# One hybrid-attention layer on one core: every attention matmul contracts over 128 rows, by padded or doubled operands

## Chip, cores and metric

The kernel runs on one core of one Trainium2 chip. The metric is the device time of the whole program in microseconds (us), the median of several executions. Lower is better. Two versions are compared: the kernel before, and the same kernel with the change below.

## What is computed

One transformer layer, batch 1, 1024 tokens, width 1024, all in float32. The reference, cut to the lines that matter here:

```python
hn = rms_norm(x, g_mix)
proj = hn @ w_in                      # split into q, k, v of three attention kinds, a convolution, gates
# NSA, 4 heads of 64, one shared key head: compressed (63 keys) + selected + window branches
kc = rms_norm(compress_tokens(kc_tok, pe_k, w1_k, w2_k), g_kc)      # 63 keys
vc = compress_tokens(vc_tok, pe_v, w1_v, w2_v)
sc = einsum('bhqd,bnd->bhqn', qi, kc) * scale                       # ... softmax, mask
o_cmp = einsum('bhqn,bnd->bhqd', p_cmp, vc)
ss = einsum('bhqd,bqkjd->bhqkj', qi, kg) * scale                    # selected blocks
# stick-breaking attention, 4 heads of 64
z = einsum('bhqd,bhsd->bhqs', qi, k) * hd ** -0.5
attn = where(past, exp(log_sigmoid(z) - between), 0.0)              # between: sum over later keys
# dilated attention, 4 heads of 64: three dilations, mixed by their log-sum-exp
groups = rms_norm(concat([o_a, o_b, o_c, o_d]), g_out)
x = x + groups @ w_out
h2 = rms_norm(x, g_ffn)
out = x + (silu(h2 @ w_gate) * (h2 @ w_up)) @ w_down
```

## The kernel before

**Products in three passes.** Float32 products run as fast fp32r matmuls: an operand a is split into a high part (rounded, one copy on ACT) and a low part (the rest, one subtraction on DVE or POOL), and a product is hi·hi + hi·lo + lo·hi, three matmuls into one PSUM bank (lines 235 to 237, in `mm3`).

**Stages.** The input is normalized and transposed; projections, a convolution and the attention kinds follow in the order `n0 n1 c0 pd0 d0 pd1 d1 ps0 s0 c1 ps1 g s1` (n: NSA, pd and d: projections and attention of the dilated kind, ps and s: of the stick-breaking kind, c: convolution, g: gains; each for head pair 0 or 1). Then come the output projection, a second norm, and the feed-forward part, which uses a seven-product scheme on half matrices. Each attention stage loops over 8 query tiles of 128 tokens (`qt`), and over chunks of up to 512 keys.

**Scores.** A head has 64 channels, so a head's query fits in half of the 128 partitions. `q_split` puts the high part of head h in its own half of `Q[h]` and the low part in the other half. `k_split` puts the high part of the key in both halves of `K[h]`, so that one matmul over 128 rows (line 496) gives q_hi·k_hi + q_lo·k_hi. The third product, q_hi·k_lo, is a second matmul over the 64 rows of that head alone (line 497): `K[2]` holds k_lo of head 0 in rows 0 to 63 and of head 1 in rows 64 to 127. For NSA, with one shared key head, `K[2]` holds the low part of the key in both halves, and line 497 also takes only 64 of the rows. `HALF` are the two slices of 64 rows.

**The compressed branch** has 63 keys. Its scores (line 662) go through DVE (line 515), the softmax (ACT line 622, then DVE or POOL line 630), a transpose of 63 columns for each head (line 669), a split (lines 522 and 523), and two matmuls over 63 rows with the values `vcHL` (lines 671 and 672).

**After the scores** the weights of a tile are transposed (lines 542 and 544), split (522 on ACT, 523 on DVE) and multiplied with the values (550 and 551). A helper `qk_pair` takes both SP buffers of PSUM for the two heads of a chunk; ten S2 buffers hold score tiles.

**Order.** `fix_order` plans the order of the instructions on each engine with a list scheduler and pins it. Its table of durations gives every fp32r matmul of n columns the same duration, whatever its rows; a DMA ends about 2 us after its issue there. Projection matmuls of the next stages stand between the attention's matmuls on TensorE (PE). SyncE (SP) issues nearly all DMAs, in its planned order: weight loads `raw`, half copies of keys (line 317), masks and distance tables `W` and `Wsp`, stores `mixd`.

Of the kernel before, what the change touches and what calls it, by code (L numbers as in the profile page):

```python
# [9 lines left out]
F32 = mybir.dt.float32  # L10
F32R = mybir.dt.float32r
# [28 lines left out]
WHB = 12  # L40
# [8 lines left out]
def hybrid(ctx, tc, x, gmix, wa1, wa2, wkv, wcv, wd, wc, bgate, gcols, pe, w1, w2,  # L49
           convw, gout, wout, gffn, wgate, wup, wdown, c_wa, c_wsp, c_wd, c_wc, c_ind, out):  # L50
    nc = tc.nc
# [11 lines left out]
    nc.scalar.preload_act_table_set("natural_log_exp_and_others")  # L63
    ident = cst.tile([128, 128], F32, name="ident")
    make_identity(nc, ident)
    if WARM:
# [19 lines left out]
    nc.vector.memset(blk1r[64:128, 64:128].bitcast(F32), 1.0 / HD)  # L86
    identr = cst.tile([128, 128], F32R, name="identr")
    nc.vector.tensor_copy(identr, ident)
    gates = cst.tile([128, NT, 12], F32, name="gates")
# [44 lines left out]

    # ---------------------------------------------------------------- attention pools
    att = ExitStack()
# [6 lines left out]
    def S2(name="S"):  # L143
        return sm.tile([128, 512], F32, tag="S2", bufs=10, name=name)

    wct = sm.tile([128, 4, 120], F32, tag="wct", bufs=1, name="wct")

# [241 lines left out]

    # ---------------------------------------------------------------- NSA projections  # L390
    ks, kw = qktile("ks"), qktile("kw")
# [30 lines left out]
    ks, kw = (ks[0],) + ks, (kw[0],) + kw  # L422
    for dst, src in ((pet, pe), (wct, c_wc), (go, gout), (cvw, convw)):
        nc.sync.dma_start(dst, src)

    # ---------------------------------------------------------------- compression
    KK, VV = Stile(), Stile()
# [12 lines left out]
    kcT = cst.tile([128, 64], F32, name="kcT")  # L440
    vcHL = cst.tile([64, 128], F32R, name="vcHL")
    for z, src in ((0, KK), (1, VV)):
# [46 lines left out]

    # ---------------------------------------------------------------- attention pieces  # L490
    def qk_pair(Q, K, qt, c0, n, diag=None):
        ps = [SPt(), SPt()]
        qc = slice(qt * 128, (qt + 1) * 128)
        kc_ = slice(c0, c0 + n)
        for h in range(2):
            nc.tensor.matmul(ps[h][:, :n], Q[h][:, qc], K[h][:, kc_], start=True, stop=False)  # L496
            nc.tensor.matmul(ps[h][:, :n], Q[h][HALF[h], qc], K[2][HALF[h], kc_], start=False, stop=diag is None)  # L497
        if diag is not None:
            b = max(0, diag - 128)
            for h in range(2):  # L500
                nc.tensor.matmul(ps[h][:, b:b + 256], identr, tri_[0][:, b + 128 - diag:b + 384 - diag],
                                 start=False, stop=True)
        return ps

    def chunks(j0, L):
# [8 lines left out]
    def reduce_min(S, ps, W, mm, first):  # L514
        nc.vector.tensor_tensor_reduce(S, ps, W, op0=OP.add, op1=OP.min, scale=1.0,  # L515
                                       scalar=3e38 if first else mm, accum_out=mm)
# [85 lines left out]
    def attn_nsa(hp, Q):  # L602
        Wt = [sm.tile([128, T], F32, tag="W", bufs=2, name="W") for _ in range(2)]
        Wsp = [sm.tile([128, 128], F32, tag="Wsp", bufs=2, name="Wsp") for _ in range(2)]
        for h in range(2):
            nc.sync.dma_start(Wt[h], c_wa[2 * hp + h])
            nc.sync.dma_start(Wsp[h], c_wsp[2 * hp + h])
        for qt in range(NT):
# [50 lines left out]
            mm, ll = small()  # L659
            Sc = sm.tile([128, 2, 64], F32, tag="Sc", bufs=2, name="Sc")  # L660
            for h in range(2):
                nc.tensor.matmul(ps[h][:, :63], f(Q[h][:, qc]), kcT[:, :63], start=True, stop=True)
            for h in range(2):
                reduce_min(Sc[:, h, :63], ps[h][:, :63], wct[:, 2 * hp + h, 8 * (7 - qt):8 * (7 - qt) + 63],
                           mm[:, h:h + 1], True)
            norm(0, [[Sc[:, 0, :63]], [Sc[:, 1, :63]]], mm, ll)
            tp = Ttile()
            for h in range(2):
                nc.tensor.transpose(tp[:63, h * 128:(h + 1) * 128], Sc[:, h, :63], ident)
            ph, pl = evac_T(tp, [(63, 0, 256)])  # L670
            nc.tensor.matmul(o[:, :256], vcHL[:63, :], ph[:63, :256], start=True, stop=False)
            nc.tensor.matmul(o[:, :256], vcHL[:63, :], pl[:63, :256], start=False, stop=False)
            five = [(j0, 384, 384), (j0 + 384, 256, 256)]
# [20 lines left out]
    def attn_dil(hp, Q, K, V):  # L694
# [3 lines left out]
        for qp in range(NT // 2):  # L698
# [4 lines left out]
            for j in range(2):  # L703
                qt = 2 * qp + j
                L = 128 * (qt + 1)
                w0 = 128 * (7 - qt)
                chs = chunks(0, L)
                for ci, (c0, w, n) in enumerate(chs):
                    ps = qk_pair(Q, K, qt, c0, n)
                    for h in range(2):  # L710
                        P[h, j, ci] = S2()
                        reduce_min(P[h, j, ci][:, :w], ps[h][:, :w], Wt[h][:, w0 + c0:w0 + c0 + w],
                                   mm[:, 2 * h + j:2 * h + j + 1], ci == 0)
                for h in range(2):
                    i = 2 * h + j
                    for ci, (c0, w, n) in enumerate(chs):
                        S = P[h, j, ci][:, :w]
                        nc.scalar.activation(S, S, AF.Exp, bias=mm[:, i:i + 1], scale=-1.0,
                                             accum_out=ll[:, 4 * ci + i:4 * ci + i + 1])
# [19 lines left out]
    def attn_stick(hp, Q, K, V):  # L739
        for qp in range(NT // 2):  # L740
            P = {}
            car = {}
            for ci in range(qp // 2, -1, -1):
                for j in range(2):
# [3 lines left out]
                    diag = ci == qp // 2  # L748
                    ps = qk_pair(Q, K, qt, c0, max(256, w), w - 128 if diag else None)
                    for h in range(2):  # L750
# [17 lines left out]

    # ---------------------------------------------------------------- short convolution
    def conv(i):  # L770
# [61 lines left out]

    # ---------------------------------------------------------------- output projection, second norm
    x2d = [[dram.tile([128, 512], F32, name=f"x2d{t}{h}") for h in range(2)] for t in range(NT)]
# [152 lines left out]

    # ---------------------------------------------------------------- gate and up
    npf = [0]
# [82 lines left out]

    # ---------------------------------------------------------------- down
    NI = NF // 2
# [15 lines left out]
    first = {}  # L1090
# [90 lines left out]

# ---------------------------------------------------------------- issue order
#
# The engines take their instructions in order, so an instruction that is not ready holds up everything
# behind it. fix_order() plans the order of the traced instructions with a list scheduler (each engine
# takes the first instruction in program order that can start) and pins it with same-engine edges. It
# only picks an order: every wait still comes from the tile framework.

# [349 lines left out]
```

## Time and profile before

| | us |
|---|---|
| median of three runs | 1395.58 (1393.94 to 1396.36) |
| profiled execution, first to last instruction | 1392.6 |
| PE busy in it | 1357.9 (98%) |
| DVE busy | 1020.2 (73%) |
| ACT busy | 739.5 (53%) |
| POOL busy | 590.0 (42%) |
| mean granted TensorE clock | 0.998 of full speed |

All times below are from this one execution and count from its first instruction. The page gives no more of its own time than the span of 1392.6 us, which is 3.0 us under the median of the runs. PE's busy time counts matmuls from their start to a modelled end, and several are in flight at once; how fast PE really goes is read from the distance between the starts of matmuls that follow each other. PEld is the weight load of a matmul, which may run beside the matmul ahead of it. NSA runs from about 100 to 315 us, the dilated attention from 315 to 455 us, and the stick-breaking attention from 455 to 680 us; what follows has no 64-row matmul.

### The profile page before, as it was taken

To read this page: it belongs to the slowest core of one execution; us is meant where nothing else is said; L and a number is where in the kernel's file an instruction comes from. 1 tells how busy PE (TensorE), PEld (TensorE's weight loads), DVE (VectorE), ACT (ScalarE), POOL (GpSimd) and SP (SyncE) were. 2 spreads that over 40 slices of the span, in tenths; PEclk is the share of its full clock that TensorE was granted. 3 is DMA by queue.
4 is the path that set the end of the run, shared out by engine and by line. 5 is a ranking of instruction groups with operands and counts; after the bars stand their busy time and mean duration, and the time that the engine had idled before them with its cause. 6 is when DMAs were issued, how large, how long until landed. Compare 5 with 4: busy or idle time off the path is not lost.

```text
span 1392.6 us, 20585 instructions
## 1 busy us (share of the span) xinstructions
PE 1357.9 (98%) x7101; PEld 1102.9 (79%) x7101; DVE 1020.2 (73%) x1985; ACT 739.5 (53%) x1643; POOL 590.0 (42%) x457
## 2 busy tenths in 40 slices
PE   7999999999999999999989999999999999999998
PEld 6997778878777776888987888888888887888786
DVE  6647778788887777788768778775766665679963
ACT  6436577676766778777765432333332323632531
POOL 5413255442311104252377334453444433564845
PEclk9999999999999999999999999999999999999999
DMA  6510011011121102451345444433233325963434
GB/s 217 171 61 5 5 41 63 15 43 50 46 57 43 39 8 76 129 159 61 127 149 187 144 164 161 144 120 99 91 107 114 114 88 196 335 210 109 138 90 158
DMA packets 84136, 150.96 MB, mean 108 GB/s; under 512 B 8960, under 2 KB 30336, under 8 KB 84032
## 3 DMA queue, kind: packets, MB, share of 16 engines
q1 hardware_dynamic: 83472, 147.82, 32.4%
q0 software_dynamic: 560, 1.84, 0.4%
q8 instruction: 56, 0.92, 0.3%
q14 instruction: 48, 0.39, 0.1%
HBM read 111.08 MB, written 36.44 MB: 106 GB/s over the span
## 4 chain that ended last, share of the span: by engine, by line
PE 83%; DVE 10%; DMA 2%; ACT 2%; issue 2%; POOL 1%; SPq 0%; DVEq 0%; POOLq 0%; ACTq 0%
PE PRp L237 9%; PE PRp L236 9%; PE PRp L235 9%; PE SPp L497 5%; PE PRp L1026 3%; PE PRp L1024 3%; PE PRp L1025 3%; PE SPp L496 3%; PE Op L550 2%; PE Op L551 2%; PE Tp L1026 2%; PE SPp L1025 2%; PE Tp L1025 2%; PE SPp L1026 2%; PE SPp L1024 2%; PE Tp L1024 2%
## 5 line engine op out<-in xcount | busy, mean ns | idle before, releaser
L104 POOL TENSOR_TENSOR wlo<-raw,whi 128x512 fp32r<-128x512 f32 x86 | 118.4, 1386 | 150.5 <-ACT whi L103 108.2
L1013 POOL TENSOR_TENSOR fw<-fraw,fw 128x512 fp32r<-128x512 f32 x50 | 68.6, 1372 | 158.2 <-ACT fw L1012 158.1
L523 DVE TENSOR_TENSOR ptl<-Tp,pth 128x512 fp32r<-128x512 f32 (+2 forms) x204 | 106.2, 533 | 31.9 <-ACT pth L522 29.4
L522 ACT ACTIVATE pth<-Tp 128x512 fp32r<-128x512 f32 (+2 forms) x204 | 93.4, 473 | 68.0 <-PE Tp L544 51.3
L1012 ACT ACTIVATE fw<-fs 128x512 fp32r<-128x512 f32 x88 | 53.4, 630 | 132.9 <-DVE fs L1003 109.0
L1083 DVE TENSOR_TENSOR fw<-sraw,fw 128x512 fp32r<-128x512 f32 x73 | 92.0, 1282 | 28.0 <-ACT fw L1082 27.7
L630 POOL TENSOR_SCALAR S<-S,ll 128x256 f32<-128x256 f32 (+3 forms) x48 | 59.2, 1240 | 98.1 <-DVE ll L627 39.2
L1083 POOL TENSOR_TENSOR hw<-bB,hw 128x512 fp32r<-128x512 f32 x55 | 81.3, 1493 | 45.2 <-ACT hw L1082 44.9
L236 PE MATMUL PRp<-XL,whi 128*128 128x512 f32 x224 | 93.0, 415 | 0.0
L235 PE MATMUL PRp<-XH,whi 128*128 128x512 f32 x224 | 92.1, 411 | 0.0
L237 PE MATMUL PRp<-XH,wlo 128*128 128x512 f32 x224 | 92.1, 411 | 0.0
L1013 DVE TENSOR_TENSOR fw<-fs,fw 128x512 fp32r<-128x512 f32 x88 | 75.7, 880 | 15.7 <-ACT fw L1012 15.6
L237 PE MATMUL PRp<-whi,ML 128*128 128x256 f32 (+1 forms) x248 | 71.3, 290 | 0.9 <-DVE ML L792 0.9
L235 PE MATMUL PRp<-whi,MH 128*128 128x256 f32 (+1 forms) x248 | 71.2, 289 | 0.1
L236 PE MATMUL PRp<-wlo,MH 128*128 128x256 f32 (+1 forms) x248 | 70.9, 287 | 0.0
L544 PE MATMUL Tp<-ident,S 128*128 128x128 f32 x292 | 67.8, 273 | 1.2 <-DVE S L727 1.2
L542 PE MATMUL Tp<-ident,S 128*128 128x128 f32 x260 | 67.4, 276 | 1.2 <-DVE ptl L523 1.0
L1082 ACT ACTIVATE hw<-bB 128x512 fp32r<-128x512 f32 x62 | 39.0, 629 | 53.4 <-PE Op L237 22.0
L103 ACT ACTIVATE whi<-raw 128x512 fp32r<-128x512 f32 x86 | 53.0, 617 | 24.5 <-PE PRp L236 17.3
L622 ACT ACTIVATE S<-S,mm 128x384 f32<-128x384 f32 (+3 forms) x96 | 55.9, 585 | 10.9 <-DVE mm L515 8.7
L1012 ACT ACTIVATE fw<-fraw 128x512 fp32r<-128x512 f32 x50 | 31.4, 627 | 57.0 <-DMA fraw<-in_wup_dram 26.7
L583 POOL TENSOR_TENSOR sl<-tk,sh 128x256 fp32r<-128x256 f32 x24 | 18.9, 788 | 94.7 <-ACT sh L580 92.9
(470 smaller groups left out, 4643.9 us busy)
## 6 DMA issues: line engine op xcount, KB each, us to landing
fraw<-in_wgate_dram SPq DMA_DIRECT2D x22, 512.0 KB, 4.4
fraw<-in_wup_dram SPq DMA_DIRECT2D x22, 512.0 KB, 4.3
bB<-in_wdown_dram SPq DMA_DIRECT2D x44, 256.0 KB, 4.5
sraw<-hS SPq DMA_DIRECT2D x44, 256.0 KB, 2.7
raw<-in_wout_dram SPq DMA_DIRECT2D x30, 256.0 KB, 2.9
hS<-s SPq DMA_DIRECT2D x30, 256.0 KB, 2.1
sraw<-hA SPq DMA_DIRECT2D x29, 256.0 KB, 3.8
xt<-in_x_dram SPq DMA_DIRECT2D x8, 512.0 KB, 10.2
```

Source lines behind the costliest of these rows:

```text
L104: (lo or nc.gpsimd).tensor_tensor(dst_lo, raw, f(dst_hi), op=OP.subtract)
L235: nc.tensor.matmul(ps, a[0], b[0], start=first, stop=False)
L236: nc.tensor.matmul(ps, a[0], b[1], start=False, stop=False)
L237: nc.tensor.matmul(ps, a[1], b[0], start=False, stop=last)
L522: nc.scalar.activation(ph[:rows, c0:c1], tp[:rows, c0:c1], AF.Copy)
L523: nc.vector.tensor_tensor(pl[:rows, c0:c1], tp[:rows, c0:c1], f(ph[:rows, c0:c1]), op=OP.subtract)
L1012: nc.scalar.activation(wt[:, 0, :], a, AF.Copy)
L1013: eng.tensor_tensor(wt[:, 1, :], a, f(wt[:, 0, :]), op=OP.subtract)
L1024: nc.tensor.matmul(ps, wt[:, 0, c], bh[:, k, :], start=k == 0, stop=False)
L1025: nc.tensor.matmul(ps, wt[:, 0, c], bl[:, k, :], start=False, stop=False)
L1026: nc.tensor.matmul(ps, wt[:, 1, c], bh[:, k, :], start=False, stop=k == 3)
L1083: eng.tensor_tensor(wt[:, 1, :], raw, f(wt[:, 0, :]), op=OP.subtract)
```

## The change

- `qk_pair`: the second score matmul now takes all 128 rows. For NSA it multiplies the whole of `Q[h]` (high and low part) with `K[2]`, whose two halves are the same. For the other two kinds the query comes from a new tile `zq` [128, 2, 128], in which head h has its high part in its own half and zeros in the other.
- `zero_padded` makes that tile: two tiles for the whole kernel, cleared once by POOL, and for each query tile of the dilated and the stick-breaking kind two DMAs of 64 x 128 from `Q` (64 DMAs in all, on SP). The tile of `qt` is used again by `qt + 2`.
- The compressed branch: the two score tiles `Sc` [128, 192] are cleared once and kept, head 0 in columns 0 to 62 and head 1 in 64 to 126; each head's transpose takes 128 columns, and `vcHL` has 128 rows, of which rows 63 to 127 are zero, so the value matmuls contract over 128 rows.
- Buffers: `zq` takes the memory of the `Sc` tiles (tag `pad0`, `pad1`), one identity serves both the fp32 and the fp32r use, and the table `wct` is loaded by head pair (two DMAs, in place of one).

```diff
+    identr = cst.tile([128, 128], F32R, name="ident")
+    ident = identr.bitcast(F32)
+    idf = main.tile([128, 536], F32, tag="whl", bufs=WHB, name="idf")[:, :128]
+    make_identity(nc, idf)
+    nc.vector.tensor_copy(identr, idf)
...
-    vcHL = cst.tile([64, 128], F32R, name="vcHL")
+    vcHL = cst.tile([128, 128], F32R, name="vcHL")
+    nc.gpsimd.memset(f(vcHL), 0.0)
+    SCB = []
+    for i in range(2):
+        z = sm.tile([128, 192], F32, tag=f"pad{i}", bufs=1, name=f"Sc{i}")
+        nc.gpsimd.memset(z, 0.0)
+        SCB.append(z)
...
-    def qk_pair(Q, K, qt, c0, n, diag=None):
+    def qk_pair(Q, K, qt, c0, n, diag=None, Z=None):
...
-            nc.tensor.matmul(ps[h][:, :n], Q[h][HALF[h], qc], K[2][HALF[h], kc_], start=False, stop=diag is None)
+            q2 = Q[h][:, qc] if Z is None else Z[:, h, :]
+            nc.tensor.matmul(ps[h][:, :n], q2, K[2][:, kc_], start=False, stop=diag is None)
...
+    ZQ = []
+
+    def zero_padded(Q, qt):
+        if not ZQ:
+            for i in range(2):
+                ZQ.append(sm.tile([128, 2, 128], F32R, tag=f"pad{i}", bufs=1, name="zq"))
+                nc.gpsimd.memset(f(ZQ[i]), 0.0)
+        z = ZQ[qt % 2]
+        for h in range(2):
+            nc.sync.dma_start(f(z[HALF[h], h, :]), f(Q[h][HALF[h], qt * 128:(qt + 1) * 128]))
+        return z
...
+        wct = sm.tile([128, 2, 120], F32, tag="wct", bufs=1, name="wct")
+        nc.sync.dma_start(wct, c_wc[:, 2 * hp:2 * hp + 2, :])
...
-                nc.tensor.transpose(tp[:63, h * 128:(h + 1) * 128], Sc[:, h, :63], ident)
-            ph, pl = evac_T(tp, [(63, 0, 256)])
-            nc.tensor.matmul(o[:, :256], vcHL[:63, :], ph[:63, :256], start=True, stop=False)
-            nc.tensor.matmul(o[:, :256], vcHL[:63, :], pl[:63, :256], start=False, stop=False)
+                nc.tensor.transpose(tp[:, h * 128:(h + 1) * 128], Sc[:, h * 64:h * 64 + 128], ident)
+            ph, pl = evac_T(tp, [(128, 0, 256)])
+            nc.tensor.matmul(o[:, :256], vcHL, ph[:, :256], start=True, stop=False)
+            nc.tensor.matmul(o[:, :256], vcHL, pl[:, :256], start=False, stop=False)
...
# attn_dil, in the loop over qt
+                Z = zero_padded(Q, qt)
-                    ps = qk_pair(Q, K, qt, c0, n)
+                    ps = qk_pair(Q, K, qt, c0, n, Z=Z)
...
# attn_stick, in the loop over pairs of query tiles
+            Z = [zero_padded(Q, 2 * qp + j) for j in range(2)]
-                    ps = qk_pair(Q, K, qt, c0, max(256, w), w - 128 if diag else None)
+                    ps = qk_pair(Q, K, qt, c0, max(256, w), w - 128 if diag else None, Z[j])
```

The planned order, at two places. On PE, in the stick-breaking attention, at a chunk of 512 keys (SPp are score banks, ckh and ckr the high part of the keys and `K[2]`, PRp a projection). Before:

```order
L236 MATMUL PRp<-XL,whi 128x512
L496 MATMUL SPp<-ckh,cqh 128x512
L497 MATMUL SPp<-ckr,cqh 128x512
L501 MATMUL SPp<-tri,identr 128x256
L237 MATMUL PRp<-XH,wlo 128x512
```

and with the change (the same statements have slightly other line numbers there):

```order
L235 MATMUL PRp<-XL,whi 128x512
L501 MATMUL SPp<-ckh,cqh 128x512
L503 MATMUL SPp<-ckr,zq 128x512
L507 MATMUL SPp<-tri,ident 128x256
L236 MATMUL PRp<-XH,wlo 128x512
```

The second score matmul reads `zq` in place of the query itself; its place among the projections is the same.

On SP, where NSA ends and the dilated attention begins (raw are weights for coming projections, dkh and dkl the half copies of keys, W the distance tables). Before:

```order
L127 DMA raw<-in_wd_dram 128x4x128 x2
L127 DMA raw<-in_wc_dram 128x4x128
L317 DMA dkl<-dkl 64x512
L593 DMA mixd<-MO 128x256
L127 DMA raw<-in_wc_dram 128x4x128
L317 DMA dkh<-dkh 64x512
L127 DMA raw<-in_wc_dram 128x4x128
L317 DMA dkl<-dkl 64x512
L697 DMA W<-in_c_wd_dram 128x1024 x2
```

and with the change:

```order
L128 DMA raw<-in_wd_dram 128x4x128 x2
L128 DMA raw<-in_wc_dram 128x4x128 x2
L316 DMA dkl<-dkl 64x512
L611 DMA mixd<-MO 128x256
L520 DMA zq<-dqh 64x128
L520 DMA zq<-dql 64x128
L128 DMA raw<-in_wc_dram 128x4x128
L316 DMA dkh<-dkh 64x512
L717 DMA W<-in_c_wd_dram 128x1024
```

The copies into `zq` stand among the weight loads and the key copies; the first pair is ahead of a weight load, and further pairs stand ahead of and between the two loads of W.

## Rows read from the trace of the kernel before

**Rows 1.** The page's busy times: engine, us, share of the span, instructions.

```profile
PE 1357.9 (98%) x7101; PEld 1102.9 (79%) x7101; DVE 1020.2 (73%) x1985; ACT 739.5 (53%) x1643; POOL 590.0 (42%) x457
```

**Rows 2.** Busy time of each engine in the three attention stages and in what follows: the stretch in us, its length, then busy us (and instructions) of PE, PEld, DVE, ACT, POOL, the granted clock, the DMA share and GB/s.

```profile
100.00:315.00 215.00, 214.48 (x1211) 163.91 (x1210) 166.29 (x593) 147.59 (x418) 91.95 (x86) 1.00 0.10 28
315.00:455.00 140.00, 137.20 (x797) 108.41 (x796) 109.85 (x314) 97.62 (x252) 30.64 (x26) 1.00 0.17 49
455.00:680.00 225.00, 217.81 (x1281) 177.74 (x1280) 178.22 (x335) 172.28 (x368) 68.23 (x52) 1.00 0.28 86
680.00:1392.60 712.60, 698.77 (x3163) 568.16 (x3161) 508.25 (x622) 275.60 (x497) 359.09 (x255) 1.00 0.43 145
```

**Rows 3.** The timeline of PE around one score pair of the stick-breaking attention: start in us, duration in us, line, tiles out<-in, rows*columns of the weights, shape.

```profile
511.00 0.40 PE L496 MATMUL SPp<-ckl,cql 128*128 128x512 f32 x1
511.32 0.50 PE L497 MATMUL SPp<-ckr,cql 64*128 64x512 f32 x1
511.75 0.50 PE L237 MATMUL PRp<-XH,wlo 128*128 128x512 f32 x1
512.08 0.39 PE L235 MATMUL PRp<-XH,whi 128*128 128x512 f32 x1
512.31 0.39 PE L236 MATMUL PRp<-XL,whi 128*128 128x512 f32 x1
```

**Rows 4.** The weight loads of the same stretch, in the same form; in brackets the idle time of the weight path before one.

```profile
510.77 0.19 PEld L496 LDWEIGHTS SPp<-ckl,cql 128*128 128x128 f32 x1
511.32 0.18 PEld L497 LDWEIGHTS SPp<-ckr,cql 64*128 64x128 f32 x1 [0.36 <-issue]
511.75 0.19 PEld L237 LDWEIGHTS PRp<-XH,wlo 128*128 128x128 f32 x1 [0.24 <-issue]
511.86 0.19 PEld L235 LDWEIGHTS PRp<-XH,whi 128*128 128x128 f32 x1
```

**Rows 5.** The timeline of PE around a score pair of 256 keys in NSA.

```profile
250.04 0.28 PE L496 MATMUL SPp<-ksh,q23l 128*128 128x256 f32 x1
250.25 0.38 PE L497 MATMUL SPp<-ksl,q23l 64*128 64x256 f32 x1
250.56 0.39 PE L236 MATMUL PRp<-wlo,XH 128*128 128x256 f32 x1
250.78 0.28 PE L237 MATMUL PRp<-whi,XL 128*128 128x256 f32 x1
250.90 0.28 PE L235 MATMUL PRp<-whi,XH 128*128 128x256 f32 x1
```

**Rows 6.** The windows view of line 497 alone, in the three attention stages: length, busy us of PE and of PEld with the number of instructions.

```profile
100.00:315.00 215.00, 40.33 (x94) 17.18 (x94) 1.00 0.10 28
315.00:455.00 140.00, 22.25 (x50) 9.14 (x50) 1.00 0.17 49
455.00:680.00 225.00, 21.48 (x48) 8.77 (x48) 1.00 0.28 86
```

**Rows 7.** The same view of line 671 alone, over the whole span (line 672 has the same count).

```profile
0.00:1392.60 1392.60, 6.01 (x16) 2.93 (x16) 1.00 0.33 108
```

**Rows 8.** The timeline of PE around the value matmuls of the compressed branch.

```profile
210.67 0.28 PE L237 MATMUL PRp<-whi,XL 128*128 128x256 f32 x1
210.88 0.38 PE L671 MATMUL Op<-pth,vcHL 63*128 63x256 f32 x1
211.10 0.28 PE L672 MATMUL Op<-ptl,vcHL 63*128 63x256 f32 x1
211.31 0.38 PE L550 MATMUL Op<-pth,VA 128*128 128x256 f32 x1
211.53 0.28 PE L236 MATMUL PRp<-wlo,XH 128*128 128x256 f32 x1
```

**Rows 9.** The longest wait of PE in the stick-breaking attention: line and what it waited for, us in total, times, the longest.

```profile
PE SPp L496 <- DVE car L764: 2.1, 2, 1.4
```

**Rows 10.** The 35 us stretches with the busiest DVE, one in the attention and one in the feed-forward part, in the form of rows 2.

```profile
280.00:315.00 35.00, 34.97 (x196) 26.31 (x195) 30.34 (x97) 25.97 (x70) 16.66 (x15) 1.00 0.14 40
1260.00:1295.00 35.00, 33.89 (x146) 26.93 (x145) 34.73 (x39) 12.67 (x23) 18.30 (x12) 1.00 0.27 80
```

**Rows 11.** The copies of half keys: the time SP takes to issue one (ns, least/median/most), and the DMA view's size and median us from issue to landing.

```profile
L317 SPq DMA_DIRECT2D dkh<-dkh x4: 467/468/522, 259.0 to 402.1; - x4
dkh<-dkh SPq DMA_DIRECT2D x4, 128.0 KB, 2.2
```

**Rows 12.** Small operations: a memset on POOL, a multiplication of compressed scores on POOL (ns, least/median/most), the load of a 64 KB table (KB, median us to landing), and the longest wait of PE for the first transposes (us in total, times, the longest).

```profile
L733 POOL MEMSET tri<- x1: 526/526/526, 449.5 to 449.5; 128x512 f32 x1
L630 POOL TENSOR_SCALAR Sc<-Sc,ll x16: 458/462/494, 105.8 to 307.2; 128x63 f32<-128x63 f32 x16
Wsp<-in_c_wsp_dram SPq DMA_DIRECT2D x4, 64.0 KB, 2.1
PE Tp L190 <- DVE xn L179: 8.0, 2, 7.5
```

**Rows 13.** The weight loads of the two score matmuls (ns, least/median/most).

```profile
L496 PEld LDWEIGHTS SPp<-dkh,dqh x24: 186/188/190, 321.4 to 446.8; 128*128 128x128 f32 x24
L497 PEld LDWEIGHTS SPp<-dkr,dqh x24: 182/183/183, 321.7 to 447.8; 64*128 64x128 f32 x24
```

**Rows 14.** The timeline of PE where two 64-row matmuls of different halves follow each other.

```profile
247.21 0.49 PE L497 MATMUL SPp<-ksl,q23l 64*128 64x512 f32 x1
247.22 0.38 PE L672 MATMUL Op<-ptl,vcHL 63*128 63x256 f32 x1
```

More of the change, by code (lines that the diff above doesn't have):

```diff
@@ L63, in hybrid @@
     nc.scalar.preload_act_table_set("natural_log_exp_and_others")
-    ident = cst.tile([128, 128], F32, name="ident")
-    make_identity(nc, ident)
+    identr = cst.tile([128, 128], F32R, name="ident")
[3 more added lines that the diff above has]
+    nc.vector.tensor_copy(identr, idf)
     if WARM:
@@ L86, in hybrid @@
     nc.vector.memset(blk1r[64:128, 64:128].bitcast(F32), 1.0 / HD)
-    identr = cst.tile([128, 128], F32R, name="identr")
-    nc.vector.tensor_copy(identr, ident)
     gates = cst.tile([128, NT, 12], F32, name="gates")
@@ L144, in S2 @@
         return sm.tile([128, 512], F32, tag="S2", bufs=10, name=name)
-    wct = sm.tile([128, 4, 120], F32, tag="wct", bufs=1, name="wct")
     def Ttile():
@@ L422, in hybrid @@
     ks, kw = (ks[0],) + ks, (kw[0],) + kw
-    for dst, src in ((pet, pe), (wct, c_wc), (go, gout), (cvw, convw)):
+    for dst, src in ((pet, pe), (go, gout), (cvw, convw)):
         nc.sync.dma_start(dst, src)
@@ L659, in attn_nsa @@
             mm, ll = small()
-            Sc = sm.tile([128, 2, 64], F32, tag="Sc", bufs=2, name="Sc")
+            Sc = SCB[qt % 2]
             for h in range(2):
@@ L663, in attn_nsa @@
             for h in range(2):
-                reduce_min(Sc[:, h, :63], ps[h][:, :63], wct[:, 2 * hp + h, 8 * (7 - qt):8 * (7 - qt) + 63],
+                reduce_min(Sc[:, h * 64:h * 64 + 63], ps[h][:, :63], wct[:, h, 8 * (7 - qt):8 * (7 - qt) + 63],
                            mm[:, h:h + 1], True)
-            norm(0, [[Sc[:, 0, :63]], [Sc[:, 1, :63]]], mm, ll)
+            norm(0, [[Sc[:, 0:63]], [Sc[:, 64:127]]], mm, ll)
             tp = Ttile()
             for h in range(2):
-                nc.tensor.transpose(tp[:63, h * 128:(h + 1) * 128], Sc[:, h, :63], ident)
-            ph, pl = evac_T(tp, [(63, 0, 256)])
-            nc.tensor.matmul(o[:, :256], vcHL[:63, :], ph[:63, :256], start=True, stop=False)
-            nc.tensor.matmul(o[:, :256], vcHL[:63, :], pl[:63, :256], start=False, stop=False)
+                nc.tensor.transpose(tp[:, h * 128:(h + 1) * 128], Sc[:, h * 64:h * 64 + 128], ident)
+            ph, pl = evac_T(tp, [(128, 0, 256)])
+            nc.tensor.matmul(o[:, :256], vcHL, ph[:, :256], start=True, stop=False)
+            nc.tensor.matmul(o[:, :256], vcHL, pl[:, :256], start=False, stop=False)
             five = [(j0, 384, 384), (j0 + 384, 256, 256)]
```

## The prediction

> **What bounds the kernel now.** I read the busy times first: PE is busy 98% of the span, no other engine more than 73% [rows 1]. Then the same by stage: in each attention stage PE is busy 97 to 100%, DVE 77 to 79% and ACT 69 to 77% [rows 2], so the attention lasts as long as PE needs. Busy time does not tell what PE does with it, since the recorded matmuls overlap. So I went to the timeline and took differences of starts. Between full-height matmuls of 512 columns the starts lie 0.23 us apart (512.08 to 512.31), and the next weights are loaded while a matmul runs (the load at 511.86 falls into the matmul of 511.75) [rows 3, 4]. Around a 64-row matmul this breaks down: its own weight load starts only with it, after 0.36 us of idle weight path, and the load for its successor again starts only with the successor, after 0.24 us [rows 4]. Nothing that the profile shows is waited for there. The bound is thus PE, and part of PE's time is the change between heights.
>
> **Price of one 64-row matmul among full ones.** With 512 columns [rows 3]: the matmul ahead takes 0.32 us (511.00 to 511.32), itself 0.43, its successor 0.33; less three times 0.23 that is 0.09 + 0.20 + 0.10 = 0.39 us too much. With 256 columns [rows 5]: 0.21, 0.31 and 0.22 against 0.12, so 0.09 + 0.19 + 0.10 = 0.38 us. The excess does not depend on the columns; I take 0.385 us.
>
> **The change part by part.**
>
> The second score matmul goes to 128 rows, with the same columns and the same place in the order. There are 94 + 50 + 48 = 192 [rows 6]. Removed: 192 x 0.385 = 74 us, namely 36 in NSA, 19 in the dilated and 19 in the stick-breaking stage. What it becomes costs 0.23 us at 512 columns, which the full matmuls around it show.
>
> The value matmuls of the compressed branch, 16 pairs [rows 7]: where both stand together, the four distances 0.21, 0.22, 0.21 and 0.22 exceed 0.12 by 0.38 us in all [rows 8]; where something stands between them it is a price for each, 0.77. The 16 pairs cost 6 to 12 us; I take 8, since the pair shown is together. Both terms: 74 + 8 = 82 us of PE, on the path that sets the end.
>
> The trace shows the opposite of this price in one place: a 64-row score matmul and a 63-row value matmul that lie in opposite halves start at 247.21 and 247.22, so they run together [rows 14]. The Trainium skill, TensorE: Matmul & The Clock Gate, Part 3 (Packing small matmuls), makes this a rule against this change: products with few rows should be put in separate row groups, where they run concurrently. If the 96 pairs of heads did that now, padding would take back 96 x 0.23 = 22 us, and the sum below would be 38 in place of 60. In the rows the first product of the other head or a projection stands between them [rows 3, 5], so I put nothing.
>
> What is late next: waits for DVE and ACT. If all 82 us went, NSA would last 215 - 44 = 171 us, the dilated stage 121 and the stick-breaking one 206. DVE's busy time would then be 166.3/171 = 97%, 91% and 86% of them [rows 2]. Lower bound of the new waits: 0, since DVE does reach 99% of a stretch (34.73 of 35) in the feed-forward part; a gain is excluded, because nothing is taken from DVE. Upper bound: DVE gets no busier than in its best attention stretch, 30.34/35 = 87% [rows 10]. Then NSA lasts 191 us and the dilated stage 126, so 20 + 5 = 25 us are lost, and the third stage loses next to nothing. I take 18, nearer to the upper one: a score tile goes PE, DVE, ACT, DVE, PE, and in the stick-breaking stage such a chain already makes PE wait up to 1.4 us at a time [rows 9].
>
> The copies into `zq`: 64 DMAs of 32 KB. A pair takes SP 2 x 0.47 us to issue and 2.2 us to land [rows 11], 3.1 us. It can start when the tile two query tiles back has been read. In the new order the matmuls between that reading and the next use are worth 3.6 us (one case) to 21 us, counted with 0.12 and 0.23 us each [rows 3, 5], so the cover is the other query tile and the projections. Bounds: 0, and 32 tiles x 3.1 = 100 us if the cover is gone. I take 3 us: the first tile of each of the four stages late by under 1 us. Behind a copy that waits stand weight loads and the tables W on SP; SP spends 64 x 0.47 = 30 us more on issuing, and its DMA engines are 10 to 28% busy in these stages [rows 2].
>
> The rest, 1 us together. Three memsets on POOL before the compressed branch and two before the dilated stage, at most 0.53 us each, beside a POOL that works 92 of 215 us [rows 2, 12]. The second `wct` load waits for the last score of head pair 0 and lands some 2.1 us later [rows 12]; 77 rows of PE's order stand in between, over 9 us. Both compressed transposes now need the POOL product of head 1 (0.46 us [rows 12]); before, the split behind them needed it as well. The 32 transposes have 128 columns in place of 63: at most 32 x 0.12 = 4 us if each took a slot more, 0 taken, because the moving side stays 128 columns. The first transposes now wait for the copied identity too, but they wait up to 7.5 us for the normalized input [rows 12].
>
> The feed-forward part is untouched: PE 698.8 of 712.6 us [rows 2]. It starts earlier, with a shift of a few us either way where weight splits meet it.
>
> Sum: 82 - 18 - 3 - 1 = 60 us. The span of 1392.6 becomes 1332.6, and with the 3.0 us by which the median of the runs is longer than this span, 1336 us.
>
> **Rivals.**
>
> DVE binds at its present level. If the in-order chains hold DVE at 79% of a stage, its most so far [rows 2], NSA lasts 166.3/0.79 = 210 us, the dilated stage 139 and the stick-breaking one 225: a gain of 6, less 3 for the copies, 1393 us. Anything between this and the forecast is possible. For it: all three stages sit at 77 to 79%. Against: PE is the one that is full there, so 79% is what PE asked for, and a stretch has 87% [rows 10].
>
> The height is not the cause. If the slow starts came from something else about line 497 (its second operand, or adding onto the bank just written), the padded form would keep them. The weight loads themselves speak for it, 183 ns at 64 rows and 188 at 128 [rows 13]. Against: the value matmuls, with other operands, show the same excess [rows 8], and projections add onto one bank at 0.23 [rows 3]. Then the time is 1396 to 1400 us with the copies. The same page of the Trainium skill (LDWEIGHTS, and the table Why this matters for your kernels) says that load time goes by columns alone and that a single matmul with few rows takes as long as a full one; by that rule the gain would be 0, which is this case, and the trace agrees on the load but not on the distance of starts.
>
> The copies set the pace (slower). Each tile's score product waits for its 3.1 us of issue and landing because SP holds the copy behind something that waits: 32 x 3.1 = 100 us against 82 saved, so 1396 + 100 - 82 = 1414 us. It decides from 82/32 = 2.6 us of exposed wait for a tile on. For it: SP takes its queue in order, and copies stand among key copies and weight loads. Against: the cover above, 3.6 us at the least.
>
> **How the numbers follow.** About 0.2% (3 us) is what a measurement of this kernel can tell from no change. Forecast, 1312 to 1366 us: 0.80. It runs from all 82 us kept (1392.6 - 82 + 3, less 2 for a shift in the feed-forward part) to waits of 42 us with copies of 10 and the rest at 1 (a gain of 29). Faster, but over 1366 (DVE binds): 0.08. Faster still than 1312: 0.03. Height not the cause: 0.05, of which 0.04 within 0.2%. Copies set the pace: 0.04. So faster 0.91, same 0.04, slower 0.05. The range 1312 to 1366 leaves out 2 in 10 and is the likeliest case's own.
>
> **What would show it.** Right: the starts around the second score matmul at 0.23 (512 columns) and 0.12 (256), its weight load begun during the matmul ahead, with no idle weight path before it; NSA shorter by 30 to 44 us, the other two stages by 10 to 19 each; DVE over 85% of NSA; the feed-forward part as long as before. Wrong: distances of 0.3 and more still there (height not the cause); PE waiting for DVE or ACT by tens of us (DVE binds); PE waiting for the copies at score products, or SP queued at them for long with weight loads behind (copies set the pace).

## The result and the profile after

| | before | after |
|---|---|---|
| median, us | 1395.97 (4 runs) | 1334.24 (1333.74 to 1334.6, 4 runs) |
| ratio, 95% interval | | 0.956 (0.9547 to 0.9574) |
| span of the profiled execution, us | 1392.6 | 1332.3 |

The change takes 61.7 us off; 60 were forecast, and 1336 us. The windows view of the changed kernel, cut where the three attention stages and the rest now lie (columns as in [rows 2]; the cuts are those of [rows 2], moved to about the same count of matmuls):

```profile
100.00:285.00 185.00, 180.52 (x1231) 162.10 (x1230) 166.09 (x593) 146.02 (x417) 92.94 (x87) 1.00 0.12 36
285.00:407.00 122.00, 118.97 (x785) 105.78 (x784) 108.41 (x313) 95.82 (x253) 31.22 (x27) 1.00 0.23 62
407.00:620.00 213.00, 201.40 (x1274) 175.94 (x1273) 177.07 (x337) 172.44 (x370) 69.13 (x51) 1.00 0.31 94
620.00:1332.30 712.30, 700.32 (x3171) 569.81 (x3169) 506.15 (x621) 274.00 (x497) 358.50 (x257) 1.00 0.43 145
```

Against [rows 2] NSA went from 215 to 185 us, the dilated stage from 140 to 122, the stick-breaking one from 225 to 213; the rest takes as long as before. DVE does the same work in less time (166 us in both NSA stages), so its share of NSA rises from 77% to 90% (78 to 89% and 79 to 83% in the other two).

The timeline of PE at a score pair of the stick-breaking attention, which answers to [rows 3]:

```profile
440.67 0.39 PE L234 MATMUL PRp<-XH,whi 128*128 128x512 f32 x1
440.91 0.40 PE L235 MATMUL PRp<-XL,whi 128*128 128x512 f32 x1
441.14 0.48 PE L501 MATMUL SPp<-ckl,cql 128*128 128x512 f32 x1
441.46 0.40 PE L503 MATMUL SPp<-ckr,zq 128*128 128x512 f32 x1
441.70 0.28 PE L599 MATMUL Tp<-sh,blk1r 128*128 128x256 f32 x1
441.82 0.28 PE L507 MATMUL SPp<-tri,ident 128*128 128x256 f32 x1
```

and its weight loads, which answer to [rows 4]:

```profile
441.12 0.19 PEld L501 LDWEIGHTS SPp<-ckl,cql 128*128 128x128 f32 x1 [0.26 <-DVE S L787]
441.23 0.19 PEld L503 LDWEIGHTS SPp<-ckr,zq 128*128 128x128 f32 x1
441.46 0.19 PEld L599 LDWEIGHTS Tp<-sh,blk1r 128*128 128x128 f32 x1
```

The second score matmul (line 503) now takes 0.24 us from start to start, in place of 0.43, and what follows it keeps its own distance (0.12 for 256 columns). Its load begins at 441.23, while the matmul of 441.14 runs. The 0.32 us of line 501 here is another thing: its load waited 0.26 us for a result of DVE.

Where did the time go? I added up, over the three stages, how much the distance from each matmul's start to the next exceeds that of a full matmul of its width (0.232, 0.175, 0.118 us for 512, 384, 256 columns). At a matmul of 63 or 64 rows, the one ahead of it and the one behind it, at most 0.2 us each is counted as price. That price is 82.2 us before and nothing after. All other excess, which is mostly waits, is 30.5 us before (9.1, 7.0 and 14.4 by stage) and 49.6 after (18.7, 9.5 and 21.4). The distances behind matmuls of 128 and 63 columns, transposes above all, are 61.4 us before and 64.7 after. So 82.2 us went, 19.1 and 3.3 came back, and 59.8 of the 60 us by which the three stages are shorter are told.

Two of the longest waits of PE in the attention after (us in total, times, the longest), and of its weight path:

```profile
PE SPp L501 <- DVE S L787: 4.3, 8, 1.2
PE Op L569 <- DVE ptl L541: 3.8, 5, 1.5
```

```profile
PEld Op L569 <- DVE ptl L541: 8.1, 15, 2.0
PEld SPp L501 <- DVE S L787: 7.4, 14, 1.5
PEld SPp L501 <- issue: 5.6, 6, 2.3
```

They name score tiles and split weights from DVE; the row with "issue" names nothing, and its longest case is looked at below. In the whole list of PE's waits no copy into `zq` stands. SP itself did queue at them, 113 us in all before a tile was free (the costliest row is the first below), with weight loads behind; no loss of PE by it is seen. A copy takes 0.46 us to issue and 1.8 us in the median to land, where 2.2 was assumed, and 4.7 at most:

```profile
SPq L520 <- PE SPp L503: 40.8, 23, 4.3
L520 SPq DMA_DIRECT2D zq<-cqh x16: 461/467/467, 389.3 to 582.7; - x16
DMA to landing us min/median/max: 1.7/1.8/4.7
```

### The profile page after: what moved, and what is told of

Same layout as the page of the kernel before. It is cut to its first block, busy times and chain, and to the rows that moved or that the text cites. A ratio compares the mean times of both kernels' runs of the same rounds, so it can differ in the third digit from the quotient of the medians.

```text
span 1332.3 us, 20737 instructions
## 1 busy us (share of the span) xinstructions
PE 1288.0 (97%) x7101; PEld 1095.4 (82%) x7101; DVE 1016.1 (76%) x1985; ACT 734.2 (55%) x1643; POOL 590.5 (44%) x462
## 4 chain that ended last, share of the span: by engine, by line
PE 75%; DVE 13%; DMA 4%; ACT 4%; issue 2%; POOL 1%; SPq 1%; DVEq 0%; ACTq 0%; POOLq 0%
PE PRp L234 8%; PE PRp L236 8%; PE PRp L235 8%; PE PRp L1048 4%; PE PRp L1046 4%; PE PRp L1047 4%; PE SPp L1048 2%; PE Tp L1047 2%; PE SPp L1047 2%; PE SPp L1046 2%; PE Tp L1048 2%; PE Tp L1046 2%; PE Op L569 2%; PE SPp L501 2%; PE Op L568 2%
## 5 line engine op out<-in xcount | busy, mean ns | idle before, releaser
L541 DVE TENSOR_TENSOR ptl<-Tp,pth 128x256 fp32r<-128x256 f32 (+1 forms) x204 | 106.2, 532 | 16.1 <-ACT pth L540 14.4
L540 ACT ACTIVATE pth<-Tp 128x256 fp32r<-128x256 f32 (+1 forms) x204 | 93.1, 472 | 41.8 <-PE Tp L562 28.6
L235 PE MATMUL PRp<-XL,whi 128*128 128x512 f32 x224 | 89.5, 400 | 0.0
```

Of the source, the lines that this page charges most:

```text
L235: nc.tensor.matmul(ps, a[0], b[1], start=False, stop=False)
L540: nc.scalar.activation(ph[:rows, c0:c1], tp[:rows, c0:c1], AF.Copy)
L541: nc.vector.tensor_tensor(pl[:rows, c0:c1], tp[:rows, c0:c1], f(ph[:rows, c0:c1]), op=OP.subtract)
```

## Experiments

### Undo the height alone

The changed kernel with all its copies, buffers and its order on every engine; only the operands of the matmuls go back to 64 and 63 rows.

```diff
-            q2 = Q[h][:, qc] if Z is None else Z[:, h, :]
-            nc.tensor.matmul(ps[h][:, :n], q2, K[2][:, kc_], ...)
+            q2 = Q[h][HALF[h], qc] if Z is None else Z[HALF[h], h, :]
+            nc.tensor.matmul(ps[h][:, :n], q2, K[2][HALF[h], kc_], ...)
...
+    # transposes of 63 columns, vcHL[:63, :] and ph[:63, :256] in the compressed branch
```

> The changed kernel in all its buffers, copies and its order on every engine, but with the 64 rows (63 in the compressed branch) back in the matmuls: only the height is undone. Theory (the height of a matmul is the price, about 0.385 us each): the time goes back to the kernel before plus the price of the copies, 1394 to 1404 us. Rival (the new planned order made the gain): 1334 to 1345 us. Rival (the copies cost much and hide part of a larger gain): over 1406 us.

Measured: 1395.85 us, ratio to before 0.9997 (0.9984 to 1.0009). The whole gain is gone, in the order of the changed kernel, so the order did not make it, and the copies with all the new buffers cost nothing that can be measured while PE is the bound (the interval is 2.2 us less to 1.3 us more). The distances are back; PE's timeline of this kernel at a score pair:

```profile
513.24 0.40 PE L501 MATMUL SPp<-ckl,cql 128*128 128x512 f32 x1
513.57 0.50 PE L503 MATMUL SPp<-ckr,zq 64*128 64x512 f32 x1
514.00 0.50 PE L236 MATMUL PRp<-XH,wlo 128*128 128x512 f32 x1
514.34 0.39 PE L234 MATMUL PRp<-XH,whi 128*128 128x512 f32 x1
514.57 0.39 PE L235 MATMUL PRp<-XL,whi 128*128 128x512 f32 x1
```

Starts 0.33, 0.43, 0.34 and then 0.23 us apart: the 0.39 us of [rows 3], with `zq` as the operand.

### The price alone, in the feed-forward part

The changed kernel, with one matmul of every twelve in the gate and up products on 64 rows: 138 of them, in a stage with few waits. The order on every engine is that of the changed kernel. Half of that term is left out there.

```diff
-                nc.tensor.matmul(ps, wt[:, 0, c], bl[:, k, :], start=False, stop=False)
+                r = slice(0, 64 if k == 1 else 128)
+                nc.tensor.matmul(ps, wt[r, 0, c], bl[r, k, :], start=False, stop=False)
```

> The changed kernel, but in the gate and up products of the feed-forward part one matmul of every twelve (138 in all, the second one of k = 1) contracts over 64 rows, so half of that term is left out there; no other work changes. It puts the price alone into a stage in which PE runs at 0.23 us a matmul and waits for nothing. Theory (a 64-row matmul among full ones costs 0.39 us more than a full one, wherever it stands): 1334 + 138 x 0.39 = 1388 us (1384 to 1392). Rival (the price belongs to the score matmul, its bank or its operands): 1334 to 1340 us. Rival (fewer rows are cheaper): under 1332 us.

Measured: 1385.96 us, 51.7 us over the changed kernel, 0.375 us for each of the 138. Less work in the array, and more time. The timeline of PE in this kernel:

```profile
1101.17 0.40 PE L1049 MATMUL PRp<-T,fw 128*128 128x512 f32 x1
1101.40 0.40 PE L1046 MATMUL PRp<-T,fw 128*128 128x512 f32 x1
1101.73 0.49 PE L1048 MATMUL PRp<-T,fw 64*128 64x512 f32 x1
1102.15 0.50 PE L1049 MATMUL PRp<-T,fw 128*128 128x512 f32 x1
1102.49 0.40 PE L1046 MATMUL PRp<-T,fw 128*128 128x512 f32 x1
```

The matmuls of one such product all add onto one bank; only the height differs. The rival that blames the score matmul's bank or operands is out.

### The parts

Three kernels that keep one part of the change, or leave one out.

```diff
# nsa_scores_only: rows by kind, no copies, compressed branch on 63 rows
+            r = slice(0, 128) if Z is None else HALF[h]
+            nc.tensor.matmul(ps[h][:, :n], Q[h][r, qc], K[2][r, kc_], ...)
# dil_stick_only: the other way round, with zq; compressed branch on 63 rows
+            r = HALF[h] if Z is None else slice(0, 128)
+            q2 = Q[h][r, qc] if Z is None else Z[:, h, :]
# compressed_63: the changed kernel with the compressed branch on 63 rows
```

> Only the second NSA score matmul takes 128 rows (94 of 192); the dilated and the stick-breaking kind and the compressed branch have 64 and 63 rows, and there are no copies. Theory: 36 us of PE go, of which a fifth to a third returns as waits: 1364 to 1372 us. Rival (DVE binds in NSA, which is its densest stage): over 1380 us.

> Only the dilated and the stick-breaking kind have the 128-row second product, with the copies into zq (98 of 192); NSA has 64 and 63 rows. Theory: 38 us of PE go, less a quarter in waits and 3 us for the copies: 1364 to 1373 us. With the run of NSA alone and the one without the compressed padding the three gains add up to that of the whole change within 6 us. Rival (the copies take much of the gain): over 1378 us.

> The changed kernel, but the compressed branch transposes 63 columns and contracts over 63 rows as before; scores stay at 128 rows. Theory: 16 pairs at 0.38 to 0.77 us come back, 8 us of PE, of which some lies in waits: 1338 to 1344 us. Rival (the compressed branch has no price, since its pairs stand together): 1333 to 1336 us.

| kernel | us | ratio, interval | what follows |
|---|---|---|---|
| NSA scores only | 1369.15 | 0.9806 (0.9791 to 0.9821) | 27.1 us off the 1396.27 beside it, of 36 in PE's sum |
| dilated and stick-breaking only | 1368.67 | 0.9806 (0.9791 to 0.9821) | 27.6 us off, of 38 |
| all but the compressed branch | 1337.98 | 0.959 (0.9571 to 0.9609) | 3.7 us over the whole change, of 8 |

The first two lie in their theory's range, the third at the low end of it. 27.1 + 27.6 + 3.7 = 58.4 us against 61.7 for all: the parts add up, within the 6 us that were expected. Each keeps about three quarters of its price, except the small one, which keeps half. The stage that DVE fills most (NSA) loses no more of it than the others, so a DVE that binds at its old level is out.

### Opposite halves side by side

The kernel before, 64 rows kept, with a planner that is told to put the two heads' second score matmuls directly behind each other (77 of 96 pairs then stand so). This tests the case that speaks against the change: that products on opposite halves run together and so should keep their 64 rows.

```diff
         for h in range(2):
             nc.tensor.matmul(ps[h][:, :n], Q[h][:, qc], K[h][:, kc_], start=True, stop=False)
+        for h in range(2):
             nc.tensor.matmul(ps[h][:, :n], Q[h][HALF[h], qc], K[2][HALF[h], kc_], ...)
...
+        if op.eng == "PE" and any(not a.write and a.ap[0][1] == 64 and a.n == 128 for a in acc):
+            op.deps.add(op.n - 1)
```

> The kernel before, 64 rows kept, but the second score matmuls of the two heads (opposite halves of the rows) are planned directly behind each other; 77 of 96 pairs stand so. Theory A (opposite halves run together, as the one place in the trace of the kernel before): a pair pays one entry, one slot and one exit, 0.62 us in place of 1.23, so 77 x 0.6 = 46 us of PE go, and a quarter returns as waits: 1357 to 1366 us. Theory B (same height saves one change, but they run one after the other): 77 x 0.3 to 0.38 = 26 us of PE: 1371 to 1380 us. Theory C (no gain from order): over 1388 us. In none of them does it beat the padded kernel (1334 us).

Measured: 1407.36 us, ratio 1.0087 (1.0059 to 1.0116). The pair does what theory A said; PE's timeline:

```profile
400.83 0.40 PE L496 MATMUL SPp<-dkl,dql 128*128 128x512 f32 x1
401.16 0.50 PE L498 MATMUL SPp<-dkr,dqh 64*128 64x512 f32 x1
401.16 0.50 PE L498 MATMUL SPp<-dkr,dql 64*128 64x512 f32 x1
401.59 0.50 PE L237 MATMUL PRp<-XH,wlo 128*128 128x512 f32 x1
401.92 0.28 PE L582 MATMUL Tp<-sh,blk1r 128*128 128x256 f32 x1
```

Two products in 0.43 us, and with entry and exit 1.09 us (400.83 to 401.92) for four matmuls that take 0.93 as full ones: 0.16 us of price for the pair, where two apart cost 0.77. Every such pair in the trace starts within 6 ns. The time falls under theory C's "over 1388 us", but not for its reason, for the order did gain something first. The rows of the attention in this kernel (the first two together are NSA and the dilated stage), of what follows it, and of a stretch in the stick-breaking stage:

```profile
100.00:293.00 193.00, 188.63 (x1127) 149.30 (x1126) 157.04 (x560) 135.35 (x389) 85.11 (x80) 0.99 0.09 28
293.00:442.00 149.00, 143.87 (x887) 117.25 (x886) 124.53 (x348) 109.21 (x281) 38.58 (x34) 1.00 0.19 53
442.00:685.00 243.00, 220.72 (x1311) 183.71 (x1309) 179.10 (x328) 171.46 (x361) 67.12 (x52) 0.95 0.25 78
685.00:1404.90 719.90, 700.98 (x3119) 567.64 (x3117) 505.19 (x624) 277.62 (x502) 355.16 (x254) 0.98 0.43 143
...
587.60:601.30 13.70, 9.91 (x38) 8.40 (x39) 10.11 (x23) 8.38 (x20) 2.62 (x3) 0.50 0.69 239
```

and PE's wait for a score tile of DVE there, in the kernel before and in this one:

```profile
PE SPp L496 <- DVE S L765: 1.4, 3, 0.7
PE SPp L496 <- DVE S L766: 13.6, 13, 3.4
```

Up to 442 us PE has done 1127 + 887 = 2014 matmuls in 342 us, where the kernel before needs 355 us for 1211 + 797 = 2008 [rows 2]: 13 us are gained there. The stick-breaking stage then takes 243 us in place of 225 and the rest 720 in place of 713, so 25 us are lost. Line 496 waits 13.6 us for score tiles of DVE, where it was 1.4 us before. The granted clock is at the lower level (0.50 is 1.2 GHz) in several stretches behind such waits, one of them shown; the mean of 0.95 over 243 us is worth up to 12 us. The first head's score is now held back until the second head's first product has run, and the plan around it changed; which of the two makes the waits was not tested. So the concurrency is real and became time in the first two stages, and this order lost more behind them. A better order for it was not tried.

### Is it DVE's load that eats the rest?

Two ways of taking work from DVE: leave out the subtraction that makes the low part of the attention weights (the value matmul reads the high part twice), and the few memsets of that tile, which also changes the plan; then a cheaper copy in its place with the order kept. In both the low part of the weights is left out of the result.

```diff
# no_low_*: the subtraction is gone, evac_T returns ph, ph
-            nc.vector.tensor_tensor(pl[:rows, c0:c1], tp[:rows, c0:c1], f(ph[:rows, c0:c1]), op=OP.subtract)
# cheap_low*: a copy, planned with the old duration and the old reader of the bank
+            nc.vector.tensor_copy(pl[:rows, c0:c1], ph[:rows, c0:c1])
```

> The changed kernel without the subtraction on DVE that makes the low part of the attention weights (204 of them, 106 us of DVE in the trace of before); the value matmul that reads it reads the high part a second time, so PE does as much as before and the low part is left out of the result. Theory (what the change did not bring is PE waiting for the chain through DVE and ACT): a further 10 to 20 us, 1314 to 1325 us. Rival (the waits come from the copies or from elsewhere): 1329 us and more.

> The kernel before with the same subtraction left out. Theory: there PE hardly waits for DVE, so the same relief brings less than in the changed kernel: 1386 to 1396 us. Rival (the relief brings as much in both, so it says nothing on the new waits): 1376 to 1384 us.

> The changed kernel with the order on every engine kept word for word, but the subtraction on DVE that makes the low part of the attention weights is a cheaper copy of the high part (the low part is left out of the result, and the high part counts twice). The planner is told the old duration and the old reader of the bank, so only DVE's time changes, by some 40 to 60 us over the attention. Theory (what is left to PE's waits is DVE's load and the chain through it): 4 to 12 us less, 1322 to 1330 us. Rival (the waits are not DVE's): 1332 to 1336 us. That the run without the subtraction was slower would then be its other order.

> The same relief for the kernel before, in its own order. Theory: PE is full there and DVE has slack, so it brings less than in the changed kernel: 0 to 5 us, 1391 to 1396 us. Rival (the relief brings the same in both): as many us as in the changed kernel.

| kernel | us | ratio, interval |
|---|---|---|
| changed, no low part | 1344.24 | 0.9625 (0.9599 to 0.965) |
| before, no low part | 1406.68 | 1.0079 (1.0052 to 1.0106) |
| changed, cheap copy | 1338.2 | 0.9579 (0.9565 to 0.9594) |
| before, cheap copy | 1396.59 | 0.9996 (0.9986 to 1.0006) |

Three of the four miss their theory. The cheap copy in the kernel before brings 0.9 us against the 1397.48 us of the kernel before beside it, which lies within its 0 to 5 us and can't be told from nothing. Without the subtraction both kernels get 10 us slower, although DVE is busy for 85 us less in the changed one (930.7 us of 1016.1). Their PE runs at the lower clock for 17 us of the attention in the changed one and for 20 us in the other, where the same kernels with the subtraction have no such stretch there; at half clock that is worth up to 8.5 and 10 us. The windows view of one stretch, with PE busy for 5.55 of 6.90 us in 11 matmuls:

```profile
486.40:493.30 6.90, 5.55 (x11) 2.88 (x11) 3.58 (x6) 6.33 (x12) 4.79 (x4) 0.51 0.06 19
```

With the order kept, the relief changes nothing in the kernel before, and nothing for the better in the changed one. It is also smaller than meant: DVE's busy time over the three stages falls by 16 us only (160.41 + 102.24 + 173.09 against 166.09 + 108.41 + 177.07):

```profile
100.00:285.00 185.00, 181.43 (x1247) 164.76 (x1247) 160.41 (x597) 147.76 (x420) 96.95 (x88) 1.00 0.12 36
285.00:407.00 122.00, 118.77 (x783) 105.66 (x782) 102.24 (x311) 95.01 (x252) 31.51 (x27) 1.00 0.23 62
407.00:620.00 213.00, 199.89 (x1241) 173.50 (x1240) 173.09 (x333) 167.72 (x363) 66.75 (x49) 0.99 0.29 88
```

So these runs give no support to the theory that DVE's load makes the new waits, and 16 us less are too few to refute it.

The traces hold one thing more. The longest wait of PE in the changed kernel's attention ends at 561.01, just behind the DVE instruction that frees the score bank (line 787). DVE was busy all through it, with two instructions that took long beside POOL:

```profile
556.60 3.42 POOL L105 TENSOR_TENSOR wlo<-raw,whi 128x512 fp32r<-128x512 f32 x2 [2.17 <-ACT whi L104]
556.65 2.32 DVE L781 TENSOR_TENSOR_SCAN R<-one,S 128x512 f32<-128x512 f32 x1
558.89 1.41 DVE L605 TENSOR_TENSOR MO<-MO,tk 128x256 f32<-128x256 f32 x1
560.23 0.68 DVE L787 TENSOR_TENSOR S<-SPp,R 128x512 f32<-128x512 f32 x1
561.01 0.36 PE L501 MATMUL SPp<-ckh,cqh 128*128 128x256 f32 x1 [2.16 <-issue]
```

The median of line 605 is 0.42 us, and the shortest scan of line 781 with this shape takes 1.22. In this attention 31 DVE instructions take over 0.3 us more than the median of their line and shape, 19.4 us more in all. Each of the 31 runs beside an instruction of POOL, which 42% of all DVE instructions there do. PE stands still for over 0.4 us in 27 places, 22.8 us in all, and 14.0 us of it come during such a slow instruction or within about 1 us behind one. The kernel before has as many slow ones (30, 20.7 us) and less of such standing still (12.3 us). The cheaper copy made more of them (48, 33.5 us): its median is 0.42 us and its longest 1.46, which is one reason why the relief was small. No run took work from POOL, so it is likely and not shown that these slow instructions set a large part of the new waits.

### Is it the plan?

The changed kernel, with only the planner's numbers changed.

```diff
# plan_slack
-    "ACT": {"PE": 270, ...          -    "DVE": {"PE": 250, ...
+    "ACT": {"PE": 670, ...          +    "DVE": {"PE": 650, ...
# plan_measured
-            return max(53, n / 2.4) + 2.5
+            return max(53, n / 2.24) + 3
-    ... else 2.1 * n + 150
+    ... else 2.4 * n + 150
```

> The changed kernel, only the planner's hand-over times from ACT and from DVE to PE raised by 400 ns each, so that it puts more other matmuls between a result and its reader. Theory (the waits that ate a quarter of the gain are consumers placed too close behind ACT and DVE in the pinned order): 3 to 10 us less, 1324 to 1331 us. Rival (they come from the few buffers and the length of the chain itself, so another order only moves them): 1333 to 1346 us.

> The changed kernel, only the planner's durations set nearer to the trace: a matmul of 512 columns 231.6 ns in place of 215.8, of 256 columns 117.3 in place of 109.2, and a POOL subtraction of 512 columns 1379 ns in place of 1225. Theory (order is what is left): 2 to 8 us less, 1326 to 1332 us. Rival (order is not what is left): 1333 to 1346 us.

Measured: `plan_slack` 1329.65 us, ratio 0.9519 (0.9493 to 0.9544), the fastest of all; `plan_measured` 1364.65 us, ratio 0.9768 (0.9729 to 0.9806). The first is inside the theory's range, but not for the theory's reason. The last score products of the stick-breaking stage, in the changed kernel and in `plan_slack` (ns least/median/most, then the first and last start in us):

```profile
L503 PE MATMUL SPp<-ckr,zq x48: 278/366/400, 413.0 to 616.0; 128*128 128x512 f32 x24, 128*128 128x256 f32 x16, 128*128 128x384 f32 x8
```

```profile
L503 PE MATMUL SPp<-ckr,zq x48: 278/378/477, 409.9 to 616.1; 128*128 128x512 f32 x24, 128*128 128x256 f32 x16, 128*128 128x384 f32 x8
```

Both end at 616 us, so the attention gained nothing, although the order there is another one. The 3.9 us between the spans (1332.3 and 1328.4) come after it. There, as long as PE has work, the changed kernel has one stretch at the lower clock, and `plan_slack` has none (its own, of 3.4 us, lies in the attention):

```profile
697.20:704.00 6.80, 6.17 (x22) 4.81 (x22) 5.97 (x8) 2.78 (x6) 2.75 (x3) 0.50 0.22 83
```

Ahead of this stretch PE waits for the second norm (2.6 us from one matmul's start to the next at 694.0). At half the clock 6.8 us hold up to 3.4 us of loss, most of the 3.9.

`plan_measured` loses in the attention, where the excess of the starts that is no price grows from 49.6 to 78 us, and at half clock ahead of it. In that stretch PE runs 64 of the 128 matmuls of 63 columns that the compressed keys need; just ahead of it, it had waited 1.3 us for a DMA. The changed kernel runs the same 128 at the full clock, after a wait of 0.9 us, so the small matmuls alone do not explain it:

```profile
66.00:83.00 17.00, 17.00 (x81) 17.00 (x81) 2.49 (x4) 1.85 (x6) 0.00 (x0) 0.50 0.45 147
```

Numbers nearer to the trace made a worse plan. Two plans that differ a little moved this kernel by -5 and +30 us, so only pairs with one order (the height, the feed-forward part, the compressed branch, the dilated and stick-breaking part, the cheap copies) say what a small edit costs.

## Why the prediction was right

- *The bound and the price.* PE was the bound, and the change of height its price. 0.385 us for each were read from the rows; the feed-forward experiment gives 0.375 us in the time, and the undone height takes back the whole gain in the same order. The sum of 82 us stands against 82.2 found in the starts.
- *The compressed branch*, 8 us of it, brought 3.7 us of time in the run without it.
- *Waits for DVE and ACT*, 18 us: 19.1 by the starts. The total was right, and in part by luck. The upper bound of 25 us put 20 in NSA, 5 in the dilated stage and next to nothing in the stick-breaking one, by how full DVE would be; 9.6, 2.5 and 7.0 came. DVE went past the 87% that bounded it, to 90 and 89%, and the stage in which it is least full lost more than the dilated one. The mechanism is half shown: the rows name DVE's results as what PE waits for; that DVE's load sets the waits was not confirmed, since taking 16 us from it, or planning more distance, did not shorten the attention. Single slow instructions of DVE beside POOL, which the prediction did not have, are the likelier cause of many.
- *Copies into `zq`*, 3 us: mis-sized on the safe side. They cost nothing within 2 us in the kernel with the height undone; in the changed kernel they were not priced alone, but PE waits for none there. The cover of 3.6 us itself was not measured.
- *The rest*, 1 us: not told apart. About 3 us came back behind transposes and 63-column products, for which the prediction had no term.
- *By stage*: 30, 18 and 12 us came, inside the 30 to 44 and 10 to 19 that were named. DVE reached 90% of NSA, over the 85%.
- *Span and median*: 3.0 us were added; the changed kernel's median is 1.9 us over its span.
- *The rivals.* Height not the cause: out, by two runs. Copies set the pace: out, no wait for them. DVE at its old level: out, it rose to 90%. Concurrent halves: the pair does run together, and was rightly given nothing here, since one pair in the kernel before stood so (247.21 and 247.22 in [rows 14]). Its price in the prediction, 22 us off a gain of 60, was too small: a pair costs only 0.16 us more than two full matmuls at 512 columns, and by the distances of [rows 5] an estimated 0.26 at 256. With all 96 pairs side by side some 15 to 25 of the 74 us would have been there to gain.
- *The sign "SP queued at them for long"*, named for copies that set the pace, did show (113 us) without the loss. It was no sign of that by itself.

## What to carry to other kernels

Read matmuls by the distance of their starts, not by their busy time: a matmul over 64 rows among full ones cost 0.38 us more than a full one here, counted over itself and its two neighbours, and with zero or doubled operands that fill the rows it costs what a full one does. It is the change of height that costs, as far as the pairs show: two such products of 512 columns on opposite halves side by side paid 0.16 us together. The plan that put them there gained 13 us in two stages and lost more than that behind them, while filled rows won. Price an edit against a kernel with the same order on every engine, for another plan can move the time by more than the edit does.

## What was not expected

- Leaving out 204 subtractions on DVE made both kernels 10 us slower, and a planner with durations nearer to the measured ones made the changed one 30 us slower.
- DVE instructions that ran beside POOL took up to 1.1 us over their median, and none that ran alone was slow by over 0.3 us in the attention of five kernels.
- The granted clock fell to 0.50 for stretches of 3.4 to 17.1 us in the slower kernels (some 51 us in all in the one with adjacent halves); those that were looked at stand behind waits of PE. In the kernel before it fell once in mid-run, for 3.4 us, and in the changed one once, for 6.8.
- Pairs of 64-row matmuls on opposite halves and other banks started within 6 ns of each other, all that stood side by side (77 in the plan), and ran in the time of one.
